# Six of 24 adaLN parts moved from TensorE beside the mixers to ScalarE, GpSimd and VectorE in three FFNs

## The chip, the core and the metric

The kernel runs on one core of one Trainium2 chip. The metric is device time in microseconds of one execution; the kernel before took 2847.01 us (median of three runs, 2842.42 to 2851.52). In the profile PE is TensorE (PEld its weight loads), DVE VectorE, ACT ScalarE, POOL GpSimd, SP SyncE, whose queue issues the DMAs.

## The reference, cut to what matters

One inference step of a four-layer trunk over 128 context tokens and 256 latent tokens, width 1024. Layer i has a mixer (0 and 3: gated DeltaNet, GDN; 1: Mamba-2 SSD; 2: RG-LRU), then a ConvFFN with 2816 hidden channels, twice (gate and value), a 3x3 depthwise convolution and a projection back. Each of these eight sub-layers is modulated:

```python
mod = silu(cond) @ ada_w[l] + ada_b[l]                # cond: 2 rows (latents, context); ada_w[l]: 1024 x 6144
sh1, sc1, g1, sh2, sc2, g2 = jnp.split(mod, 6, -1)
x = layer_norm(ALPHA * x + g1 * mixer(x * (1 + sc1) + sh1), ln_g[0], ln_b[0])
x = layer_norm(ALPHA * x + g2 * ffn(x * (1 + sc2) + sh2), ln_g[1], ln_b[1])
```

A "part" below is one of the six 1024-wide slices of one layer's mod: two rows of 1024 inputs times a 1024 x 1024 weight. There are 24 parts, and each reads 4 MB of weights once.

## The kernel before, in words

All data is fp32. Large products run as three fp32r passes on exact high and low halves (mm3, line 157). A weight tile of 128 x 1024 (512 KB) is therefore prepared in wload (line 137): SP's queue loads it into a ring of raw buffers, ScalarE copies it to the high half (wh, or woh for the FFN's second weight), and GpSimd, sometimes VectorE, subtracts to get the low half (wl, wol). A raw buffer is free again when the subtraction is done.

**Modulation.** ada (line 187) computes one part on TensorE: for each of eight steps it loads a raw tile of 128 x 1024 and multiplies it by a 32-column slice of csilu, the SiLU of the two condition rows (the other 30 columns are zero), in plain fp32, as four products of 256 columns, one for each 32-column group of the array. They accumulate in a PSUM tile psa. At the end VectorE adds the bias (adab); a gate part is stored to a DRAM scratch (gate_rows), a shift or scale part is transposed on TensorE into a psc tile and copied out.

The 24 parts form a list, todo, that is consumed in order; HOSTED (line 28) says how many are computed beside each layer's mixer, its first boundary and its second. Two more are computed at the start. parts() (line 288) takes the next n, and more where a later sub-layer needs them. Beside a mixer the steps are spread evenly over its projections: fill (line 176) is called after each projection, at lines 761, 999 and 1319. Before, the mixers host 6 (GDN, layer 0), 3 (SSD), 3 (LRU) and 2 (GDN, layer 3) parts.

**GDN** (line 1180) advances, in turns (interleave, line 1151), 33 projections, the chain of block inversions and the chunk recurrences, so that TensorE has projections to do while a chain waits for other engines. SSD and LRU are built in the same spirit.

**A boundary** (line 297) is the end of a sub-layer: the last products, the residual and norm, and the next sub-layer's input. The norm's gain and bias are applied to x later, by affine (line 415), in half-width multiplications and additions on VectorE with both inputs in SBUF.

**The FFN** (line 547) goes through 22 slices of 128 gate and 128 value channels. In slice j, for each half: 24 products (8 slices of the input, three passes, 384 columns) into one of two psc buffers; then conv9 (line 531), one ScalarE instruction and ten of VectorE, which read the psc buffer and add into acc. In slices 1 to 6 two instructions of affine go in between. Then ScalarE's SiLU of the gate, VectorE's product g, ScalarE's high half gh, VectorE's low half gl; and out(), 18 products with the weights woh and wol of a slice three steps back, into six PSUM banks (four psa, two psb). Input weights are loaded two tiles ahead (FFN_AHEAD), through three raw buffers. The order on ScalarE is pinned to the program's order in this loop; on the other engines the framework's planner lays the order when the kernel is built, and each engine then runs its own list in order.

Of the kernel before, what the change touches and what calls it, by code (L numbers as in the profile page):

```python
# [15 lines left out]
NT = 384                       # 128 context tokens, then 256 latent tokens  # L16
# [3 lines left out]
NFF = 22                       # 128-wide slices of the FFN's hidden channels  # L20
# [3 lines left out]
FFN_AHEAD = 2                  # weight tiles loaded ahead of the one in use  # L24
FFN_LAG = 3                    # steps from a slice's first product to its last
SIDE = 4, 4, 4
FENCE = 4                      # weight tiles after a boundary that are kept behind it
HOSTED = ((6, 2, 1), (3, 2, 1), (3, 0, 1), (2, 1, 0))     # modulation parts beside each layer's mixer and norms
WBUFS = ((4, 2), (3, 4), (4, 3), (2, 6))     # raw and split weight tiles: GDN, SSD, LRU, FFN

# columns of the constant input
# [37 lines left out]
class Slices:  # L69
    """the parts of a tile that isn't in use yet, as scratch"""  # L70
# [14 lines left out]
class Trunk:  # L85
# [43 lines left out]
    def ln_exp(self):  # L129
        """one table set for both functions, so that they don't evict each other"""  # L130
        self.tables("natural_log_exp_and_others")
# [25 lines left out]
    def mm3(self, out, w, x, start, stop):  # L157
        """out += (wh + wl)^T (xh + xl) without the lo*lo pass"""
        (wh, wl), (xh, xl) = w, x
        self.mm(out, wh, xh, start, False)  # L160
        self.mm(out, wh, xl, False, False)
        self.mm(out, wl, xh, False, stop)
# [13 lines left out]
    def fill(self, share=None):  # L176
        """one step of the products hosted beside a mixer, or up to a share of them"""
# [9 lines left out]
    def ada(self, l, u, raws=None, pool=None):  # L187
        """part u of layer l's modulation (shift, scale, gate of the mixer, then of the FFN): a quarter of the
        features in each column group of the array, one row per condition"""
        nc = self.nc  # L190
# [9 lines left out]
        md = self.sb(pool or self.adap, [128, 256], "adab", 2)  # L200
# [6 lines left out]
        else:  # L207
            pc = self.ps("c")
            for s in range(2):
                self.transpose(pc[:, s * 128:(s + 1) * 128], md[:, s * 128:(s + 1) * 128])  # L210
            mc = self.modc[l, u] = self.sb(self.fix, [128, 8, 2], f"mod{u}", 2)
            nc.vector.tensor_copy(mc.rearrange("p (j s) r -> p s j r", s=2),
                                  pc[:, :256].rearrange("p (s j r) -> p s j r", s=2, j=4)[:, :, :, 0:2])
        yield

    def scales(self, l, which, ln):
        """per-feature columns A, B with h = A*n + B for n the normalized (or raw) input"""
# [30 lines left out]
    def make_h(self, t, n, A, B, pool):  # L248
        """transpose one token tile and write its hi/lo parts feature-major"""
# [18 lines left out]
    def open_bnd(self, l, which):  # L268
        """what the end of a sub-layer needs, loaded ahead"""
# [12 lines left out]
    def beside(self, l, which):  # L282
        """parts of the modulation computed at this boundary"""
        raws = (self.fp, "raw", 3) if which else (self.bp, "araw", (6, 6, 2)[l % 3])
        for part in self.parts(HOSTED[l][1 + which], () if which else ((l, 5), (l + 1, 1))):
            yield from self.ada(*part, raws, self.bp)

    def parts(self, n, need=()):
        """the next parts of the modulation to compute, at least up to those needed"""
# [7 lines left out]
    def boundary(self, l, which, pts, late, n):  # L297
        """the last products by token tile, each followed by x <- LN(alpha*x + gate*m) and the next sub-layer's
        input or the result; x stays without LN's gain and bias until affine()"""
# [25 lines left out]
        def stats(t):  # L325
            """r = alpha * x + gate * m, 1/deviation and -mean/deviation"""
# [7 lines left out]
            mv = self.sb(bp, [128, 4], "bmv", 2)      # mean, variance, 1/deviation, -mean/deviation  # L334
# [80 lines left out]
    def affine(self, lg, lb, eng=None):  # L415
        """x <- x * gain + bias of the norm before, a token tile per step"""
# [17 lines left out]
    def first_pair(self, srcs):  # L434
        """the first two products of a sub-layer, with the last token tile behind the others"""
# [17 lines left out]
    def rsqrt(self, pool, out, v, scale=1.0):  # L453
        """(scale * v + eps)^-1/2 from ln and exp, with one Newton step"""
# [9 lines left out]
    def softplus(self, pool, x, shape, tag):  # L464
        """max(x,0) + log1p(exp(-|x|)), the log1p by its atanh series"""
# [17 lines left out]
    def conv4(self, pt, dst, w, bias=None):  # L483
        """depthwise taps at offsets -1, 0, 1, 2 inside each segment"""
# [23 lines left out]
    def outproj(self, l, nk, wsrc, gety, tail=4, ws=(), swap=False):  # L508
        """the mixer's last projection, through to the FFN's input"""
# [37 lines left out]
    def ffn(self, l):  # L547
# [3 lines left out]
        with tc.tile_pool(name=self.nm("ffn"), bufs=1, reuse_waits="tile") as fp:  # L551
            self.rawp = self.fp = fp
            cw = self.sb(fp, [128, 2 * NFF, 9], "cw")
            self.load(cw, I["ffn_conv"][l])
            apool = tc.tile_pool(name=self.nm("aff"), bufs=1, reuse_waits="tile")
# [21 lines left out]
            for j in range(NFF):  # L577
                accs = []
                for half in range(2):
# [9 lines left out]
                    if j:  # L589
                        next(affine, 0)  # L590
                if j == 7:
                    apool.__exit__(None, None, None)
                if j == NFF - 3:
# [21 lines left out]
    def lru(self, l, j):  # L615
# [3 lines left out]
        with ExitStack() as es:  # L619
            op = es.enter_context(tc.tile_pool(name=self.nm("lru"), bufs=1, reuse_waits="tile"))  # L620
            Iv = self.sb(op, [128, NB, 2, NT], "I")      # input gate, then its product, then the states
# [5 lines left out]
            sm = self.sb(op, [128, NB, 8], "sm")     # gate_b x4, lambda x2, state x2  # L627
            sa = self.sb(op, [128, NB, 2], "sa")
            st = self.sb(op, [128, NB, 2], "st")
            R = None                                     # recurrence gate, then the decay  # L630
# [1157 lines left out]
```

## Time and profile before

| what | us |
|---|---|
| median of three runs | 2847.01 |
| span of the profiled execution, first to last instruction | 2845.4 |
| TensorE busy in it | 2635.5 (93%) |
| VectorE busy | 1943.4 (68%) |
| ScalarE busy | 1340.0 (47%) |
| GpSimd busy | 1283.2 (45%) |
| modulation products from raw tiles, busy union of all | 109.5 |
| mean granted TensorE clock | 0.972 |

The execution's own time is this span and the little that lies outside its first and last instruction; the median of the runs is 1.6 us above the span. The layers' FFNs lie at about 547 to 800, 1255 to 1510, 1800 to 2055 and 2558 to 2810 us, the mixers between them. In group lines, "busy" is the union over a group's instructions (matmuls overlap in the pipeline, so it is less than count times mean), then the mean of one, then the idle time of the engine just ahead and what ended it. A product in plain fp32 leaves two records in the trace, so a step of ada (four products) is eight records.

### The profile page before, as it was taken

The page shows a single profiled execution, that of the slowest core. Times are in us where ns is not written, and L with a number is a line of the kernel's source. Part 1 is how long each engine was busy: PE and PEld are TensorE (multiplying, and loading weights), DVE is VectorE, ACT ScalarE, POOL GpSimd, SP SyncE. Part 2 cuts the span into 40 slices and gives each one's busy share as a digit, 9 for nine tenths or more (in the row PEclk, how much of TensorE's full clock was granted, in tenths as well). Part 3 has the DMA queues.
Part 4 walks back from the last instruction along what each step waited for, and adds up shares of the span by engine and source line. Part 5 has one row for each costly group of instructions (what it writes and reads, how often), then busy time and mean ns, then how long its engine had stood idle before and what let it go on. Part 6 is the DMA issues. An engine that isn't in the chain of part 4 may idle for free. (4 is left out here: it accounts for less than half of the span.)

```text
span 2845.4 us, 43556 instructions
## 1 busy us (share of the span) xinstructions
PE 2635.5 (93%) x16424; PEld 2319.9 (82%) x16424; DVE 1943.4 (68%) x4200; ACT 1340.0 (47%) x2334; POOL 1283.2 (45%) x658
## 2 busy tenths in 40 slices
PE   6999998999997999899999787999989999899997
PEld 3698887799977789679997675899968888778996
DVE  3666545787786677368778776787776564578877
ACT  2455545434443566443444664344345555544443
POOL 1443332356533443335654653456545333335663
PEclk9999999999999999999999989999999999999998
DMA  7522323534454342543445443334443112053442
GB/s 260 170 96 78 107 82 103 201 132 136 148 174 143 113 127 83 188 167 127 134 148 171 160 143 114 112 128 141 160 140 91 53 57 64 30 183 119 150 137 84
DMA packets 114641, 366.45 MB, mean 129 GB/s; under 512 B 13760, under 2 KB 25728, under 8 KB 114432
## 3 DMA queue, kind: packets, MB, share of 16 engines
q1 hardware_dynamic: 114432, 363.67, 38.8%
q8 instruction: 130, 2.13, 0.3%
q14 instruction: 79, 0.65, 0.1%
HBM read 357.78 MB, written 5.84 MB: 128 GB/s over the span
## 5 line engine op out<-in xcount | busy, mean ns | idle before, releaser
L120 POOL TENSOR_TENSOR wl<-raw,wh 128x1024 fp32r<-128x1024 f32 x305 | 736.5, 2425 | 1009.7 <-ACT wh L111 974.5
L105 PE MATMUL psc<-hh,wh 128*128 128x384 f32 x2168 | 758.6, 350 | 38.5 <-DVE acc L117 14.0
L117 DVE SCALAR_TENSOR_TENSOR acc<-psc,cw,acc 128x189 f32<-128x189 f32 (+3 forms) x1680 | 646.1, 412 | 164.5 <-ACT acc L111 131.1
L105 PE MATMUL psc<-hh,wl 128*128 128x384 f32 x2168 | 736.7, 340 | 4.6 <-POOL wl L120 4.1
L105 PE MATMUL psc<-hl,wh 128*128 128x384 f32 x2168 | 735.6, 339 | 0.0
L105 PEld LDWEIGHTS psc<-hh,wh 128*128 128x128 f32 x2168 | 413.0, 190 | 83.8 <-issue 64.2
L111 ACT ACTIVATE wh<-raw 128x1024 fp32r<-128x1024 f32 x345 | 362.6, 1053 | 238.8 <-PE psc L105 53.9
L105 PEld LDWEIGHTS psc<-hh,wl 128*128 128x128 f32 x2168 | 412.3, 190 | 9.3 <-POOL wl L120 5.0
L105 PEld LDWEIGHTS psc<-hl,wh 128*128 128x128 f32 x2168 | 413.3, 191 | 8.1 <-issue 4.7
L120 POOL TENSOR_TENSOR wol<-raw,woh 128x1024 fp32r<-128x1024 f32 x88 | 211.8, 2407 | 160.4 <-ACT woh L111 159.5
L111 ACT ACTIVATE gh<-g 128x384 fp32r<-128x384 f32 x88 | 46.2, 526 | 329.2 <-DVE g L120 329.2
L111 ACT ACTIVATE acc<-psc,cw 128x384 f32<-128x384 f32 x168 | 96.6, 575 | 191.4 <-PE psc L105 191.4
L120 POOL TENSOR_TENSOR PB<-M,cst 128x512 fp32r<-128x512 f32 x96 | 128.7, 1354 | 83.3 <-PE psa L105 79.0
L111 ACT ACTIVATE V<-psa 128x512 fp32r<-128x512 f32 x144 | 85.4, 597 | 144.8 <-PE psa L105 144.4
L105 PE MATMUL psa<-woh,gl 128*128 128x512 f32 x352 | 137.1, 391 | 3.6 <-DVE gl L120 3.6
L105 PE MATMUL psa<-raw,csilu 128*32 128x256 f32 x1216 | 109.5, 422 | 32.3 <-DMA raw<-in_ada_w 32.2
L105 PE MATMUL psa<-wol,gh 128*128 128x512 f32 x352 | 137.6, 391 | 0.0
L105 PE MATMUL psa<-woh,gh 128*128 128x512 f32 x352 | 137.5, 391 | 0.1
L120 DVE TENSOR_TENSOR wl<-raw,wh 128x1024 fp32r<-128x1024 f32 x40 | 53.6, 1340 | 62.1 <-ACT wh L111 62.1
L111 ACT ACTIVATE woh<-raw 128x1024 fp32r<-128x1024 f32 x88 | 92.6, 1053 | 0.0
L105 PE MATMUL psa<-U,W 128*128 128x256 f32 x576 | 91.9, 281 | 0.0
L111 ACT ACT_TABLE_LOAD x60 | 77.0, 1283 | 28.9 <-DVE zT L117 8.1
(336 smaller groups left out, 5155.1 us busy)
## 6 DMA issues: line engine op xcount, KB each, us to landing
raw<-in_ffn_in SPq DMA_DIRECT2D x176, 512.0 KB
raw<-in_ada_w SPq DMA_DIRECT2D x152, 512.0 KB
raw<-in_ffn_out SPq DMA_DIRECT2D x88, 512.0 KB
raw<-in_gdn_in SPq DMA_DIRECT2D x66, 512.0 KB
araw<-in_ada_w SPq DMA_DIRECT2D x40, 512.0 KB
raw<-in_ssd_in SPq DMA_DIRECT2D x25, 512.0 KB
raw<-in_lru_in SPq DMA_DIRECT2D x20, 512.0 KB
raw<-in_gdn_out SPq DMA_DIRECT2D x16, 512.0 KB
```

Source lines behind the costliest of these rows:

```text
L105: return self.nc.tensor.matmul(out, l, r, start=start, stop=stop, skip_group_check=True)
L111: x = self.nc.scalar.activation(out, in_, f, scale=scale, bias=bias, **kw)
L117: return self.nc.vector.scalar_tensor_tensor(out=out, in0=a, scalar=s, in1=b, op0=op0, op1=op1)
L120: return (eng or self.nc.vector).tensor_tensor(out=out, in0=a, in1=b, op=op)
```

## The change

Six parts are taken from the mixers and computed in the FFNs of layers 0, 1 and 2, two in each, by ada_vec. An FFN does one step per slice: the whole 128 x 1024 weight tile is scaled by one condition value per partition, for each of the two conditions, and summed over the eight steps in two SBUF accumulators of 128 x 1024. The scaling is a ScalarE Copy with a scale; the sum is a GpSimd addition, or, for the second condition on odd steps, one VectorE multiply-add with both inputs in SBUF. After eight steps TensorE sums each accumulator over its 128 partitions by eight products with rowsel, a constant matrix that has ones in one column; the rest (ada_finish) is as before. The tile for the next step is loaded as soon as the current one, in a single buffer vraw, has been read. The accumulators and the scaled copy vtmp have one buffer each.

The mixers now host 3, 1, 4 and 0 parts; the boundaries host as many as before.

```diff
-HOSTED = ((6, 2, 1), (3, 2, 1), (3, 0, 1), (2, 1, 0))
+HOSTED = ((3, 2, 1), (1, 2, 1), (4, 0, 1), (0, 1, 0))
+HOSTED_FFN = 2, 2, 2, 0
...
+    def ada_vec(self, parts, pool, fp):
+        nc = self.nc
+        seq = [(l, u, k) for l, u in parts for k in range(8)]
+        def fetch(i):
+            l, u, k = seq[i]
+            raw = self.sb(pool, [128, 1024], "vraw")
+            self.load(raw, self.I["ada_w"][l, k * 128:(k + 1) * 128, u * 1024:u * 1024 + 1024])
+            return raw
+        nxt, acc = fetch(0), None
+        yield
+        for i, (l, u, k) in enumerate(seq):
+            raw = nxt
+            if k == 0:
+                acc = [self.sb(pool, [128, 1024], f"vacc{r}") for r in range(2)]
+            for r in range(2):
+                c = self.csilu[:, k, r:r + 1]
+                if k == 0:
+                    self.act(acc[r], raw, AF.Copy, c)
+                elif r == 1 and k % 2:
+                    self.stt(acc[r], raw, c, acc[r])
+                else:
+                    tmp = self.sb(pool, [128, 1024], "vtmp")
+                    self.act(tmp, raw, AF.Copy, c)
+                    self.tt(acc[r], acc[r], tmp, ALU.add, nc.gpsimd)
+            nxt = fetch(i + 1) if i + 1 < len(seq) else None
+            yield
+            if k == 7:
+                pt = self.ps("c")
+                for r in range(2):
+                    for j in range(4):
+                        self.mm(pt[32 * j:32 * j + 32, :256], self.rowsel[:, r, :], acc[r][:, j * 256:(j + 1) * 256],
+                                r == 0, r == 1)
+                self.ada_finish(l, u, pt, fp)
+                yield
...
@@ ffn
+            vparts = self.parts(HOSTED_FFN[l], () if last else ((l, 5), (self.next_layer(l), 1)))
+            vpool = tc.tile_pool(name=self.nm("adv"), bufs=1, reuse_waits="tile")
+            vp = vpool.__enter__()
+            vec = self.ada_vec(vparts, vp, fp) if vparts else iter(())
...
+                next(vec, 0)
                 if j == 7:
                     apool.__exit__(None, None, None)
+                if j == NFF - 4:
+                    for _ in vec:
+                        pass
+                    vpool.__exit__(None, None, None)
```

In slice 0 only the first tile is fetched; slices 1 to 8 do the steps 0 to 7 of the first part, slice 9 sums its partitions, slices 10 to 17 do the second part, slice 18 sums it. next(vec) stands after both halves' convolutions and ahead of the slice's woh copy. ada_finish is the end of ada, cut out unchanged; beside no longer asks for the parts that a later sub-layer needs, since ffn does.

More of the change, by code (lines that the diff above doesn't have):

```diff
@@ L187, in ada @@
     def ada(self, l, u, raws=None, pool=None):
-        nc = self.nc
         rpool, tag, n = raws or (self.wp, "raw", self.wbufs[0])
@@ L199, in ada, with ada_finish @@
                 yield
-        md = self.sb(pool or self.adap, [128, 256], "adab", 2)
+        self.ada_finish(l, u, pt, pool or self.adap)
+        yield
+    def ada_finish(self, l, u, pt, pool):
+        md = self.sb(pool, [128, 256], "adab", 2)
         self.load(md, self.I["ada_b"][l, u])
@@ L211, in ada @@
             mc = self.modc[l, u] = self.sb(self.fix, [128, 8, 2], f"mod{u}", 2)
-            nc.vector.tensor_copy(mc.rearrange("p (j s) r -> p s j r", s=2),
-                                  pc[:, :256].rearrange("p (s j r) -> p s j r", s=2, j=4)[:, :, :, 0:2])
-        yield
+            self.nc.vector.tensor_copy(mc.rearrange("p (j s) r -> p s j r", s=2),
+                                       pc[:, :256].rearrange("p (s j r) -> p s j r", s=2, j=4)[:, :, :, 0:2])
+    def ada_vec(self, parts, pool, fp):
[7 more added lines that the diff above has]
+        nxt, acc = fetch(0), None
+        yield
+        for i, (l, u, k) in enumerate(seq):
[22 more added lines that the diff above has]
+                yield
     def scales(self, l, which, ln):
@@ L284, in beside @@
         raws = (self.fp, "raw", 3) if which else (self.bp, "araw", (6, 6, 2)[l % 3])
-        for part in self.parts(HOSTED[l][1 + which], () if which else ((l, 5), (l + 1, 1))):
+        for part in self.parts(HOSTED[l][1 + which]):
             yield from self.ada(*part, raws, self.bp)
@@ L1662, in build @@
             self.act(self.csilu[:, :, 0:2], cc, AF.Silu)
+            self.rowsel = self.sb(fix, [128, 2, 32], "rowsel")
+            nc.vector.memset(self.rowsel, 0.0)
+            for r in range(2):
+                nc.vector.memset(self.rowsel[:, r, r:r + 1], 1.0)
             self.X = []
```

## The prediction

> **What bounds the kernel now.** I read the page first, then busy times by stretch, then the waits and the timeline of an FFN.
>
> ```profile
> span 2845.4 us, 43556 instructions
> PE 2635.5 (93%) x16424; PEld 2319.9 (82%) x16424; DVE 1943.4 (68%) x4200; ACT 1340.0 (47%) x2334; POOL 1283.2 (45%) x658
> PE   6999998999997999899999787999989999899997
> ```
>
> TensorE is busy for 93% of the span, and the third line shows that in nearly every fortieth. So work taken off it is worth something where nothing else ends last, and work put beside it costs nothing until another engine becomes the one that ends last. The change touches two kinds of stage, and they answer differently.
>
> *The mixers.* The two GDN layers run the same code with different numbers of hosted modulation products: six parts (48 steps of one weight tile) in layer 0, two (16 steps) in layer 3. That is an experiment already made. Below are four stretches, bounded by the third projection's first product, the eleventh projection's, and the first product of the output projection; first all instructions, then those that read the conditioning tile csilu alone. Columns are stretch, length, busy time of each engine (instructions), clock, DMA share, GB/s.
>
> ```profile
> 62.00:130.50 68.50, 62.19 (x375) 47.80 (x371) 44.03 (x101) 32.17 (x50) 25.03 (x14) 0.95 0.54 181
> 130.50:478.90 348.40, 335.15 (x2633) 297.74 (x2631) 196.56 (x457) 188.90 (x390) 123.53 (x80) 0.98 0.26 87
> 2092.70:2160.80 68.10, 56.82 (x305) 45.28 (x302) 46.51 (x92) 32.11 (x50) 41.90 (x24) 0.92 0.39 126
> 2160.80:2495.90 335.10, 319.64 (x2459) 290.93 (x2457) 193.21 (x455) 187.86 (x389) 123.97 (x81) 0.98 0.18 55
> ...
> 62.00:130.50 68.50, 7.91 (x100) 2.22 (x96) 0.00 (x0) 0.00 (x0) 0.95 0.54 181
> 130.50:478.90 348.40, 22.28 (x256) 6.96 (x256) 0.00 (x0) 0.00 (x0) 0.98 0.26 87
> 2092.70:2160.80 68.10, 3.85 (x38) 0.90 (x34) 0.00 (x0) 0.00 (x0) 0.92 0.39 126
> 2160.80:2495.90 335.10, 7.00 (x78) 1.70 (x78) 0.00 (x0) 0.00 (x0) 0.98 0.18 55
> ```
>
> A step is eight records (four fp32 products, two records each). In the long stretch layer 0 has 256 records, 32 steps; layer 3 has 78, 9.75 steps; the other PE records agree (2377 against 2381). Layer 0 takes 348.40 - 335.10 = 13.3 us longer: 13.3 / 22.25 = 0.60 us a step. In the first stretch it has 12.5 steps against 4.75 and takes 0.4 us longer: 0.05 us a step. There the steps fill holes.
>
> *The FFN.* Two stretches of layer 0's FFN: one in which VectorE also applies the last norm's gain and bias to x (affine), and one late. Then who TensorE waited for in the first.
>
> ```profile
> 585.00:636.00 51.00, 49.42 (x261) 46.10 (x260) 43.36 (x96) 19.27 (x27) 27.32 (x13) 1.00 0.35 117
> 716.00:790.00 74.00, 74.00 (x394) 69.77 (x393) 54.94 (x136) 30.21 (x43) 43.55 (x19) 1.00 0.45 146
> ...
> PE psc L105 <- DVE acc L117: 1.6, 2, 1.0
> ```
>
> Late, TensorE has no gap. In the affine stretch VectorE is busy 43.36 of 51 us, and TensorE waits 1.6 us for its convolution. The ScalarE copies gh, one a slice, show the pace:
>
> ```profile
> 589.21 0.53 ACT L111 ACTIVATE gh<-g 128x384 fp32r<-128x384 f32 x1 [4.24 <-DVE g L120]
> 628.83 0.53 ACT L111 ACTIVATE gh<-g 128x384 fp32r<-128x384 f32 x1 [6.13 <-DVE g L120]
> ...
> 743.99 0.53 ACT L111 ACTIVATE gh<-g 128x384 fp32r<-128x384 f32 x1 [3.91 <-DVE g L120]
> 756.45 0.53 ACT L111 ACTIVATE gh<-g 128x384 fp32r<-128x384 f32 x1 [3.91 <-DVE g L120]
> ```
>
> Late, a slice takes 12.46 us, set by TensorE. In the affine stretch three slices take 39.62, 13.2 each: there VectorE, with ScalarE's answers to it, already sets the pace. I expect the change to be decided in that stretch.
>
> **The change part by part.** *Taken from the mixers.* With the new counts layer 0 hosts three parts, SSD one (before: three), LRU four (three), layer 3 none (two). Layer 0: of its steps, 32 lie in the long stretch; half go, 16 x 0.60 = 9.6, and 8 early ones at 0.05, 0.4: 10.0 us. Layer 3: 9.75 x 0.60 = 5.9, and 6 early ones 0.3: 6.2 us. For SSD and LRU:
>
> ```profile
> 867.00:1100.00 233.00, 13.80 (x160) 3.49 (x160) 0.00 (x0) 0.00 (x0) 0.98 0.43 133
> 1545.00:1700.00 155.00, 15.35 (x192) 4.44 (x192) 0.00 (x0) 0.00 (x0) 0.90 0.49 158
> ...
> PE psb L108 <- DVE ys L797: 14.0, 1, 14.0
> PE psc L105 <- DVE xr L117: 13.5, 4, 5.1
> PE psa L105 <- DMA raw<-in_ada_w: 5.7, 4, 3.0
> ```
>
> SSD: 20 of its 24 steps lie after its one long wait (14.0 us, which ends at 867 and is VectorE's); two thirds go, 13.3 x 0.60 = 8.0 us; the four before the wait are worth nothing. LRU gains 8 steps. It is full of waits for VectorE (13.5 us), which hide a step, and for these very weight tiles (5.7 us), which a step lengthens; between 0.05 and 0.60 I take the middle, 8 x 0.33 = 2.6 us. Mixers together: 10.0 + 6.2 + 8.0 - 2.6 = 21.6 us less. Ends: 12, if the inversions' chain cannot use the time, and 26, if LRU's steps are free and SSD's early ones count.
>
> *TensorE's work in the FFNs.* A part ends in eight products with rowsel, the shape of two steps, back to back:
>
> ```profile
> 288.63 1.07 PE L105 MATMUL psa<-raw,csilu 128*32 128x256 f32 x16
> 289.64 0.44 PE L105 MATMUL psc<-hh,wh 128*128 128x384 f32 x1
> ```
>
> 1.0 us to the next product, six times: 6 us. The two transposes of a part move along and cancel. But the sum now takes one of the two psc buffers, and for three parts the transposes another, from the ring that feeds the convolution, and the transposes wait for VectorE's add, which is queued behind a convolution of ten instructions (nine of them here; the tenth had its own group):
>
> ```profile
> 747.05 3.90 DVE L117 SCALAR_TENSOR_TENSOR acc<-psc,cw,acc 128x127 f32<-128x127 f32 x9 [1.95 <-ACT acc L111]
> ```
>
> The output products can lie over most of that. I take 1 us a part, 6 us; ends 0 and 3.9 each.
>
> *The sixteen steps of an FFN on the other engines.* One step a slice: slices 1 to 8 and 10 to 17. The first of a part is two ScalarE products. An odd one is one ScalarE product, one GpSimd add and one VectorE multiply-add; an even one two ScalarE products and two GpSimd adds. Prices, and what happens when VectorE meets GpSimd:
>
> ```profile
> L120 POOL TENSOR_TENSOR wl<-raw,wh 128x1024 fp32r<-128x1024 f32 x305 | 736.5, 2425 | 1009.7 <-ACT wh L111 974.5
> L111 ACT ACTIVATE wh<-raw 128x1024 fp32r<-128x1024 f32 x345 | 362.6, 1053 | 238.8 <-PE psc L105 53.9
> L120 DVE TENSOR_TENSOR wl<-raw,wh x40: 1208/1225/2747, 468.2 to 2507.3; 128x1024 fp32r<-128x1024 f32 x40
> ...
> 595.49 2.40 POOL L120 TENSOR_TENSOR wol<-raw,woh 128x1024 fp32r<-128x1024 f32 x1
> 604.25 2.41 POOL L120 TENSOR_TENSOR wl<-raw,wh 128x1024 fp32r<-128x1024 f32 x1 [6.37 <-ACT wh L111]
> 745.54 4.91 POOL L120 TENSOR_TENSOR wl<-raw,wh 128x1024 fp32r<-128x1024 f32 x2 [3.39 <-ACT wh L111]
> ...
> 596.21 2.23 DVE L120 TENSOR_TENSOR x<-x,lng 128x512 f32<-128x512 f32 x1
> 601.52 0.68 DVE L120 TENSOR_TENSOR x<-x,lnb 128x512 f32<-128x512 f32 x1
> ```
>
> GpSimd's op runs from 595.49 to 597.89. VectorE's x op, both inputs in SBUF, starts inside it and takes 2.23 us; the like op at 601.52, in GpSimd's idle 6.37 us, takes 0.68. A meeting costs 1.55 us. Convolutions, which read PSUM, don't show it (the nine above took 0.43 each, mostly beside GpSimd's pair at 745.54). The Trainium skill, SBUF — State Buffer, section "SBUF: two separate sides", has the rule: the two engines share a port pair as an exclusive lock, and a VectorE op with two SBUF inputs waits out a whole GpSimd op. The trace agrees. By that rule without the slack below, every new add could be met; that is rival C.
>
> Affine slices (1 to 6) have steps 0 to 5: three odd, two even. VectorE sets the pace, so its additions count in full. Odd: 1.23 for the multiply-add and half a meeting, 2.0 us. Even: two adds fill the 6.37 us in which GpSimd stood idle and g was made unhindered: one meeting, 1.55. 3 x 2.0 + 2 x 1.55 = 9.1 us an FFN, 27 for three; ends 0 and 52 (rivals A and C).
>
> Other slices: late VectorE is busy 54.94 of 74, 3.2 us idle in a slice, over the 2.0 of an odd step. On an even step ScalarE's second product waits for the first add, since vtmp has one buffer: 2 x 1.05 + 2.4 = 4.5 us, and queued behind it stand woh, Silu, gh and the next slice's wh and acc, and TensorE behind these. Its idle 3.91 before gh nearly covers that. GpSimd then has five ops a slice and ScalarE's 1.05 between the adds, 5 x 2.4 + 1.05 = 13.1 against 12.46: 0.6 late, caught up in the odd slice after it (four, 9.6). I take 1 us an FFN, 3 in all; ends 0 and 13.
>
> The 48 weight loads go to SP's queue in the FFNs, each waiting there for its single buffer with three-buffer raw loads behind it. 66 big loads an FFN become 82: a DMA share of 0.45 becomes 0.56, about the 0.54 seen at 62 to 130 us. I cost them at nothing; if a fetch stands ahead of a needed load, up to a few us an FFN, inside C's end. The bias and gate rows move too, small and early.
>
> Sum: -21.6 + 6 + 6 + 27 + 3 = +20.4 us. On this execution's 2845.4 that is 2865.8. The median of the runs, 2847.0, is 1.6 above the span: 2867 us.
>
> **The rivals.** *A, VectorE's holes take it up, faster.* In the affine stretch VectorE idles 7.6 of 51 us, 1.9 a slice, almost what an odd step needs (2.0). If the multiply-add lies in the holes ahead of a convolution and the adds end before g, the affine term is gone, and with half the part ends: -21.6 + 6 + 3 = -12.6, 2834 us. It decides where VectorE's additions stay under 1.9 us a slice. Against it: those holes are mostly waits for ScalarE's gh and acc, in which the next op is not ready.
>
> *B, half of it.* 12 instead of 27 in the affine stretch: -21.6 + 12 + 12 = +2.4, 2849 us, not to be told from no change. For it: the order on each engine is laid anew and can part the two.
>
> *C, every two-input VectorE op meets GpSimd.* GpSimd's share in the affine stretch, 27.32 / 51 = 0.54, grows by seven adds of 2.4 in some 66 us to 0.79. Four such ops a slice and the three multiply-adds, 23, each wait 0.79 x 1.2 = 0.95: 22, less the some 8 they wait now, plus 3.7 of multiply-adds: 17.5 an FFN, 52. With late slices at 13: -21.6 + 12 + 52 + 13 = +55, 2902 us. Against it: GpSimd is idle when ScalarE waits for g, just when g runs.
>
> *D, the mixers gain half.* If the inversions become bound by their chain, 10 instead of 21.6: +32, 2879 us. Against it: 22 steps paid in full between layers 0 and 3; for it: layer 3 is then below anything seen.
>
> **How the numbers follow.** Forecast 0.40 (2867), A 0.18, B 0.25, C 0.10, D 0.07. 0.3%, 8.5 us, is about what a measurement of this kernel can tell from no change: A is faster, B the same, the others slower: 0.18, 0.25, 0.57. The range reaches from A's sum to between D and C: 2834 to 2892; outside lie most of C and A's better half.
>
> **What would show it.** Right: the GDN stretches shorter by some 10 and 6 us and SSD by 8; the three hosting FFNs each longer by 10 to 15 us, layer 3's FFN unchanged; TensorE's wait for acc in 585 to 636 up from 1.6 to about 10; g and x ops of 1.5 to 2.5 us where they took 0.6. Wrong: hosting FFNs that keep their length (A), late slices over 13 us (C), GDN stretches that don't shrink while U and W are waited for (D).

## The result and the profile after

The changed kernel takes 2935.26 us (median of four runs, 2933.72 to 2937.82); beside it, on the same chip, the kernel before took 2848.78. The ratio is 1.031, 95% interval 1.0294 to 1.0326. The direction was forecast (slower, 0.57), the size was not: 2935 lies far outside 2834 to 2892.

The head of the page and TensorE's row of the 40 slices, as shown of before:

```profile
span 2932.4 us, 43102 instructions
PE 2651.7 (90%) x16136; PEld 2342.6 (80%) x16136; DVE 2033.6 (69%) x4227; ACT 1416.3 (48%) x2406; POOL 1443.7 (49%) x718
PE   6999998989897998989989887899889999989997
```

TensorE has 288 records fewer, yet is busy 16 us longer, and its share falls from 93% to 90%. The other three engines took the work without being full: VectorE is at 69%. Where the 87 us of the span went shows when each sub-layer is measured, in the trace, from the last weights product of the one before to its own:

| us | before | after | difference | forecast |
|---|---|---|---|---|
| GDN, layer 0 | 518.7 | 514.7 | -4.0 | -10.0 |
| FFN, layer 0 | 300.0 | 335.1 | +35.1 | +14 |
| SSD | 409.0 | 392.9 | -16.1 | -8.0 |
| FFN, layer 1 | 300.0 | 335.8 | +35.8 | +14 |
| LRU | 243.3 | 250.1 | +6.8 | +2.6 |
| FFN, layer 2 | 298.9 | 329.5 | +30.6 | +14 |
| GDN, layer 3 | 467.7 | 464.9 | -2.8 | -6.2 |
| FFN, layer 3, to the end | 307.8 | 309.3 | +1.5 | 0 |

The mixers gave 16.1 us, of 21.6 forecast. The three hosting FFNs grew by 101.5, of 42 forecast: 59.5 of the 66.6 us by which the forecast missed the span's growth (87.0 against 20.4). Below are the stretches whose like was shown of before (columns as there): the affine one, the late one, and inside the late one a few us around one gap.

```profile
585.00:636.00 51.00, 45.55 (x231) 41.84 (x230) 42.05 (x82) 21.39 (x28) 38.28 (x16) 0.97 0.44 145
716.00:790.00 74.00, 61.90 (x295) 58.05 (x294) 56.90 (x115) 30.67 (x40) 55.47 (x23) 0.88 0.43 139
...
716.00:722.50 6.50, 2.00 (x9) 1.34 (x8) 6.36 (x16) 1.11 (x2) 6.50 (x4) 0.88 0.63 206
722.50:728.00 5.50, 5.50 (x18) 5.50 (x19) 3.50 (x8) 1.94 (x3) 2.51 (x2) 0.52 0.56 184
728.00:734.00 6.00, 6.00 (x35) 5.91 (x34) 3.23 (x8) 1.97 (x3) 4.11 (x2) 1.00 0.26 87
```

The late stretch, where TensorE had no gap at all, is the surprise: it is busy 61.90 of 74 us there, at a granted clock of 0.88. The last three rows show both losses. TensorE is idle for 4.5 of 6.5 us; then it is busy, but does 18 products in 5.5 us where the next 6 us hold 35: the clock is at 0.52 after the gap.

What lies ahead of that gap, engine by engine (start, us, and in brackets the idle time before and what ended it). VectorE:

```profile
709.93 1.49 DVE L121 TENSOR_TENSOR g<-acc,acc 128x384 f32<-128x384 f32 x1 [1.16 <-ACT acc L112]
712.30 2.47 DVE L118 SCALAR_TENSOR_TENSOR vacc<-vraw,csilu,vacc 128x1024 f32<-128x1024 f32 x1 [0.88 <-DMA vraw<-in_ada_w]
714.69 2.77 DVE L121 TENSOR_TENSOR gl<-g,gh 128x384 fp32r<-128x384 f32 x1
717.38 6.78 DVE L118 SCALAR_TENSOR_TENSOR acc<-psc,cw,acc 128x127 f32<-128x127 f32 x18
```

GpSimd, ScalarE's second scaled product, SP's fetch of the tile, and TensorE:

```profile
708.62 2.39 POOL L121 TENSOR_TENSOR vacc<-vacc,vtmp 128x1024 f32<-128x1024 f32 x1 [1.27 <-ACT vtmp L112]
710.97 2.71 POOL L121 TENSOR_TENSOR wol<-raw,woh 128x1024 fp32r<-128x1024 f32 x1
713.64 6.04 POOL L121 TENSOR_TENSOR wl<-raw,wh 128x1024 fp32r<-128x1024 f32 x2
...
707.38 1.16 ACT L112 ACTIVATE vtmp<-vraw,csilu 128x1024 f32<-128x1024 f32 x1 [2.52 <-POOL vacc L121]
...
708.57 0.33 SPq L135 DMA_DIRECT2D vraw<-in_ada_w  x1
...
722.50 0.66 PE L106 MATMUL psc<-hh,wh 128*128 128x384 f32 x1 [4.50 <-DVE acc L118]
```

Read it in this order. ScalarE's product waits 2.52 us for vtmp, so the next tile is only asked for at 708.57. The planner had placed the next step's multiply-add on VectorE right behind g, ahead of gl and of the next convolution; VectorE, which takes its list in order, waits there 0.88 us for the tile. Then it meets GpSimd's wol (2.47 us instead of 1.28), and gl meets wl (2.77 instead of 0.56; the kernel before has g and gl like this):

```profile
602.12 0.55 DVE L120 TENSOR_TENSOR g<-acc,acc 128x384 f32<-128x384 f32 x1
603.26 0.56 DVE L120 TENSOR_TENSOR gl<-g,gh 128x384 fp32r<-128x384 f32 x1 [0.59 <-ACT gh L111]
```

The convolution begins at 717.38, though both of ScalarE's starting values stood ready by 714.82 (the second was begun at 714.25 and took 0.57). TensorE has used up its 18 output products and waits 4.5 us for a psc buffer. None of the three delays is long. Together they are longer than what TensorE has in stock. This is one gap read closely; what the chain is worth over the whole kernel is for the experiments to say.

The same waits over this whole FFN, 520 to 850 us (total, times, longest). The first was 3.1 us, three times, in the kernel before:

```profile
PE psc L106 <- DVE acc L118: 24.7, 13, 4.6
ACT vtmp L112 <- POOL vacc L121: 17.3, 6, 3.6
DVE vacc L118 <- DMA vraw<-in_ada_w: 8.1, 5, 3.1
```

### The profile page after: what moved, and what is told of

Its sections match the earlier page's. It is cut to its first block, busy times and chain, and to the rows that moved or that the text cites. A ratio compares the mean times of both kernels' runs of the same rounds, so it can differ in the third digit from the quotient of the medians.

```text
span 2932.4 us, 43102 instructions
## 1 busy us (share of the span) xinstructions
PE 2651.7 (90%) x16136; PEld 2342.6 (80%) x16136; DVE 2033.6 (69%) x4227; ACT 1416.3 (48%) x2406; POOL 1443.7 (49%) x718
## 5 line engine op out<-in xcount | busy, mean ns | idle before, releaser
L121 POOL TENSOR_TENSOR wl<-raw,wh 128x1024 fp32r<-128x1024 f32 x305 | 747.9, 2463 | 907.4 <-ACT wh L112 873.5
L106 PE MATMUL psc<-hh,wh 128*128 128x384 f32 x2168 | 770.9, 356 | 109.1 <-DVE acc L118 76.3
L106 PE MATMUL psc<-hh,wl 128*128 128x384 f32 x2168 | 745.4, 344 | 4.8 <-POOL wl L121 4.8
L106 PE MATMUL psc<-hl,wh 128*128 128x384 f32 x2168 | 745.5, 344 | 0.0
L106 PEld LDWEIGHTS psc<-hh,wh 128*128 128x128 f32 x2168 | 421.6, 194 | 155.4 <-issue 138.9
L106 PEld LDWEIGHTS psc<-hl,wh 128*128 128x128 f32 x2168 | 421.9, 195 | 6.4 <-issue 4.4
L121 POOL TENSOR_TENSOR vacc<-vacc,vtmp 128x1024 f32<-128x1024 f32 x60 | 143.3, 2389 | 35.4 <-ACT vtmp L112 35.2
L106 PE MATMUL psa<-raw,csilu 128*32 128x256 f32 x832 | 77.6, 432 | 34.0 <-DMA raw<-in_ada_w 33.9
L121 DVE TENSOR_TENSOR gl<-g,gh 128x384 fp32r<-128x384 f32 x88 | 73.4, 834 | 41.5 <-ACT gh L112 41.5
L112 ACT ACTIVATE woh<-raw 128x1024 fp32r<-128x1024 f32 x88 | 92.5, 1051 | 13.3 <-DMA raw<-in_ffn_out 13.2
L121 DVE TENSOR_TENSOR g<-acc,acc 128x384 f32<-128x384 f32 x88 | 82.4, 936 | 16.7 <-ACT acc L112 10.6
```

What stands on the lines that cost most here:

```text
L106: return self.nc.tensor.matmul(out, l, r, start=start, stop=stop, skip_group_check=True)
L112: x = self.nc.scalar.activation(out, in_, f, scale=scale, bias=bias, **kw)
L121: return (eng or self.nc.vector).tensor_tensor(out=out, in0=a, in1=b, op=op)
```

## The experiments

Two theories stood at the start: the additions of VectorE and GpSimd meet in SBUF (L), or the single buffers vtmp and vraw make a chain of waits (B). The texts on record name further ones (T, O, S, G, H) as they came up. For all kernels below, one table of the profiled executions. It has the growth of one hosting FFN against before (mean of three), of its parts as paced by the copies gh (slice 0 to 7 "early", 7 to 18 "late"), and, per FFN, the time TensorE waited for a convolution, ran at half its clock, and VectorE stood still ahead of multiply-adds; then the change of all mixers and the last FFN together. The half clock is counted from the clock's changes in the trace, whether TensorE is busy in it or not.

| kernel | FFN | early | late | TensorE waits | half clock | VectorE waits | rest |
|---|---|---|---|---|---|---|---|
| before | 0 | 0 | 0 | 3.4 | 6.8 | 0 | 0 |
| after | +33.8 | +13.7 | +19.0 | 24.6 | 26.2 | 8.1 | -14.6 |
| a_no_sums | +2.3 | 0.0 | +1.6 | 3.3 | 5.7 | 0 | -10.0 |
| b_no_multiply_add | +15.0 | +6.7 | +8.1 | 14.2 | 6.8 | 0 | -14.0 |
| c_no_gpsimd_adds | +8.4 | +8.1 | +1.7 | 8.6 | 3.4 | 9.2 | -15.5 |
| d_two_vtmp | +28.9 | +16.7 | +13.7 | 21.8 | 19.3 | 8.0 | -15.0 |
| j_two_vraw | +44.5 | +20.3 | +28.4 | 31.8 | 42.1 | 16.7 | -9.1 |
| e_half_adds | +37.6 | +15.1 | +22.0 | 22.1 | 30.7 | 10.4 | -11.5 |
| f_all_vector | +42.8 | +23.6 | +24.6 | 32.8 | 35.3 | 9.3 | -9.7 |
| k_all_gpsimd | +35.5 | +14.4 | +19.4 | 28.7 | 15.9 | 0 | -14.9 |
| i_step_last | +33.6 | +12.4 | +29.1 | 23.0 | 23.9 | 0 | +12.3 |
| l_every_second | +25.4 | +10.4 | +13.8 | 19.0 | 20.5 | 7.8 | -8.5 |
| m_half_step | +9.0 | +4.6 | +5.2 | 8.0 | 9.1 | 5.1 | -14.8 |
| m_pinned | +16.0 | +10.4 | +13.2 | 6.2 | 10.2 | 0 | +7.7 |
| n_half_pinned | -0.4 | -0.8 | +7.3 | 1.3 | 5.7 | 0 | -0.9 |
| o_half_gpsimd | +3.2 | +1.0 | +1.4 | 4.1 | 9.1 | 0 | -2.8 |
| p_before_pinned | -5.4 | -3.1 | +2.9 | 1.0 | 3.4 | 0 | +18.8 |

A row is one execution. Those of m_half_step and n_half_pinned are the shortest of their kernels, 6 and 9 us under the median; those of o_half_gpsimd and m_pinned are the longest, 9 and 10 us above it.

**Parts of the work alone.** Without any sum beyond the first products:

```diff
-            for r in range(2):
+            for r in range(2 if k == 0 else 0):
```

> Steps 1 to 7 of the moved parts are left out (their weight tiles are still loaded, nothing reads them); step 0's two ScalarE products, the row sums on TensorE and the part ends stay. Theory L (VectorE's two-input SBUF instructions wait out GpSimd's new adds) and theory B (single buffers: ScalarE waits for vtmp, VectorE for vraw) both say that the loss goes: mixers -16, row sums +6, part ends 0 to +6, so 2837 to 2845 us. If the loads on SP's queue or the taken psc buffers were the cost, it stays above 2870.

It took 2844.51 us, a single execution as for all kernels here without an interval (before on that chip: 2852.51); its span is 2842.4, 3 below before's. What is left, loads and part ends, costs 2.3 us an FFN. So even with the sums free the change could bring no more than some 3 to 8 us.

Without the multiply-adds (their line becomes a pass), and without GpSimd's additions (their line goes):

```diff
-                    self.stt(acc[r], raw, c, acc[r])
+                    pass
...
-                    self.tt(acc[r], acc[r], tmp, ALU.add, nc.gpsimd)
```

> VectorE's multiply-add on odd steps is left out; ScalarE's products and GpSimd's adds stay. Theory L: half of the 101 us that the three FFNs grew by, since the multiply-add waits in front of gl, but g and gl still meet GpSimd: 2875 to 2895 us. Theory B: only VectorE's 8 us an FFN of waiting for vraw and the 1.2 us each go, ScalarE's wait for vtmp stays: 2900 to 2915.

> GpSimd's adds are left out; ScalarE still writes its products (nothing reads them) and VectorE keeps its multiply-adds. Theory L and B both: no new meetings and no wait for vtmp; what stays is the multiply-adds in the affine slices (3 x 2 us an FFN) and vraw: 2855 to 2875 us. If the multiply-add alone were the cost, it stays above 2900.

They took 2878.16 and 2856.89 us (2852.51). Over the floor of 2.3 the one half costs 12.7 us an FFN and the other 6.1; both together cost 31.5. Both times lie in the ranges that L gave (B gave the second's too). But the work is no sum of its parts, and neither theory said so: each half finds room that it doesn't find when the other stands there.

**The buffers.** A second vtmp, and a second vraw; in both, g has one buffer instead of two to make room, which is a change too:

```diff
-                    tmp = self.sb(pool, [128, 1024], "vtmp")
+                    tmp = self.sb(pool, [128, 1024], "vtmp", 2)
...
-            raw = self.sb(pool, [128, 1024], "vraw")
+            raw = self.sb(pool, [128, 1024], "vraw", 2)
```

> The whole computation, with two buffers for vtmp (and one for g, whose readers are done in time, to make room). Theory B: ScalarE's wait for GpSimd's add (17.3 us in one FFN) goes and with it 10 us or more an FFN: 2890 to 2905 us. Theory L: GpSimd does the same adds and VectorE meets them as before: 2920 to 2940.

> The whole computation, with two buffers for vraw (one for g), so that the next tile is loaded before ScalarE is done with the one in use. The multiply-add's waits for vraw (24 us in three FFNs) go. If that wait is what makes gl late, 2900 to 2915; if the meetings with GpSimd are, 2925 to 2940.

2918.99 (2852.51) and 2971.53 (2853.47). ScalarE's wait for vtmp is gone in the first, and the FFN is 4.9 us shorter, no more. The second is worse than the change, and above every range expected. VectorE's g starts without a wait in both, so its single buffer is not seen to cost anything. With the tile there early, VectorE waits for GpSimd's addition into the same accumulator instead; this is j's row of VectorE's waits, 550 to 860 us, and its group of multiply-adds (shortest, median, longest, ns):

```profile
DVE vacc L118 <- POOL vacc L121: 17.0, 6, 3.7
```

```profile
L118 DVE SCALAR_TENSOR_TENSOR vacc<-vraw,csilu,vacc x24: 1285/3343/3361, 556.5 to 2121.4; 128x1024 f32<-128x1024 f32 x24
```

When it may go at last, GpSimd has begun its next operation, and most multiply-adds take 3.34 us instead of 1.28. B falls as the main cause.

**The additions' shape and engine.** GpSimd's additions in two halves of 512 columns; all additions as VectorE multiply-adds; all of them on GpSimd:

```diff
-                    self.tt(acc[r], acc[r], tmp, ALU.add, nc.gpsimd)
+                    for h in (slice(0, 512), slice(512, 1024)):
+                        self.tt(acc[r][:, h], acc[r][:, h], tmp[:, h], ALU.add, nc.gpsimd)
...
-                elif r == 1 and k % 2:
+                elif True:      # f_all_vector; False: k_all_gpsimd
```

> The whole computation; each GpSimd add is cut into two of 512 columns, so GpSimd does the same work in instructions of half the length. Theory L (an instruction of VectorE with two SBUF inputs waits for the end of the GpSimd instruction it meets): the waits on g, gl and the multiply-add get shorter, the FFNs grow by 22 to 27 us each instead of 34, 2900 to 2915 us. Theory T (GpSimd's sheer load makes weights or adds late): nothing gained, 2930 to 2945.

> The whole computation; all fourteen sums of a part after step 0 are multiply-adds on VectorE, no GpSimd add and no vtmp. Theory L: the new GpSimd instructions that were met are gone, but VectorE gets 17 us a part: in the affine slices, where it sets the pace, all of it counts (10 to 15 us an FFN), in the late ones 2.5 us a slice fit into its 3.2 of idle time: 2875 to 2900 us. If VectorE's own load is what counts (four multiply-adds alone cost 8.4 us an FFN, fourteen then some 29): 2910 to 2935.

> The whole computation; all fourteen sums of a part after step 0 are GpSimd adds, no multiply-add on VectorE. Without the multiply-adds ten adds a part cost 13 us an FFN over the floor; fourteen make every slice an even one (five GpSimd instructions, 13.1 us against TensorE's 12.46): 18 to 25 us an FFN, 2895 to 2920, below the changed kernel, if the pair of multiply-add and adds is what costs. If GpSimd's load is what costs, above it: 2940 or more.

2948.61 (2849.08), 2966.10 (2849.08) and 2938.64 (2853.47): all as bad as the change or worse, the first two above every range expected. Shorter operations to wait behind don't help, nor does it to take the sums from GpSimd altogether, or from VectorE. In k ScalarE waits for vtmp instead, because GpSimd has five operations of 2.4 us in a slice that takes TensorE 12.5 (its waits, 520 to 870 us):

```profile
ACT vtmp L112 <- POOL vacc L121: 63.1, 14, 5.3
```

L alone falls too; meetings are one of several ways to be late.

**The step's place in the slice.** The step behind gl instead of ahead of woh, so that ScalarE's woh, SiLU and gh go first:

```diff
-                next(vec, 0)
...
                 self.split(gh, gl, g)
...
+                next(vec, 0)
```

> The whole computation; the step of a slice is called behind gl instead of ahead of the woh copy, so that on ScalarE its products stand behind gh, and in the program its multiply-add behind gl. Theory O (what makes the two halves cost more together than apart is the order: the multiply-add stands ahead of gl, waits for vraw and for GpSimd, and gl then meets wl): the three late TensorE waits of 3 to 4.6 us an FFN go and with them the halved clock: FFNs grow by 15 to 22 us instead of 34, 2880 to 2900. Theory L by the number of meetings alone: as many instructions meet, 2920 to 2940.

2960.20 (2853.47). This is above every range expected. Meetings of g and gl are gone but for those that before has too: the time that the 132 of them take beyond 0.56 us each is 9.7 us over the three FFNs, 57.4 in the change and 7.9 before. No multiply-add waits, and the FFN is as long as in the change: 12 early, 29 late. The multiply-adds, now in the middle of convolutions, take a median of 3.18 us, beside GpSimd nearly all the time.

**The mixers alone**, in the kernel before: two of SSD's parts, then also one of LRU's, to layer 0's GDN.

```diff
-HOSTED = ((6, 2, 1), (3, 2, 1), (3, 0, 1), (2, 1, 0))
+HOSTED = ((8, 2, 1), (1, 2, 1), (3, 0, 1), (2, 1, 0))     # g
+HOSTED = ((9, 2, 1), (1, 2, 1), (2, 0, 1), (2, 1, 0))     # h
```

> The kernel before with another distribution and nothing else: two parts that SSD hosted go to layer 0's GDN mixer (8, 1, 3, 2 beside the mixers). From the mixers of the changed kernel: SSD 14 to 16 us shorter; GDN longer by 16 steps, at 0.17 us as 24 fewer steps there showed (3 us) or at 0.60 as layers 0 and 3 showed (10 us). 4 to 13 us below the kernel before, ratio 0.995 to 0.999.

> As the other distribution, and one more part from LRU to layer 0's GDN mixer (9, 1, 2, 2). LRU grew by 6 to 13 us with 8 steps more, so with 8 fewer it may give 5 to 8; GDN takes 1.4 to 5 more. 7 to 17 us below the kernel before if LRU's price holds downwards; no better than the other one if LRU's steps only cost when they are added.

Ratios 0.9994 (0.9984 to 1.0005) and 1.0023 (1.0009 to 1.0036). The gain expected is not there: SSD is 12.6 us shorter, and GDN 11.5 longer for 16 steps more (0.72 a step). LRU is 5.1 us longer in g though it hosts what it did.

**How much in a slice.** One part in each FFN (mixers 5, 1, 3, 2): a whole step in every second slice, or half a step, one condition, in every slice.

```diff
-HOSTED_FFN = 2, 2, 2, 0
+HOSTED_FFN = 1, 1, 1, 0
...
-                next(vec, 0)
+                if j == 0 or j % 2:          # l_every_second
+                    next(vec, 0)
...
+                if r == 0:                   # m_half_step, at the end of the loop over r
+                    yield
```

> One part in each of three FFNs instead of two, a whole step in every second slice (slices 1, 3, ... 15); the mixers host 5, 1, 3 and 2 parts. Slack theory (S): a slice has some 2 to 3.5 us that nothing needs, a step costs by how far it overruns the slice it stands in, and what is overrun is lost, so a step costs what it does in the changed kernel: 31.5 us over the floor for 16 steps, 2.0 a step, 16 for 8 and 1 for the part's end: 17 us an FFN, in all 51 less 14 to 16 in SSD and 1 to 4 in layer 0: 2881 to 2889 on the time before of this chip. Lag theory (G): an overrun is made up in the next slice when that has no step: under 8 us an FFN, 2845 to 2862.

> The same parts in the same places, but half a step in a slice (one condition's product and sum, the other condition's in the next slice; 16 slices, one part). S: each half fits into the slack of its slice, as the halves alone did (6 us without GpSimd's additions, 13 without the multiply-adds, for two parts): half of these or less, 3 to 6 us an FFN with the part's end: 2838 to 2855. G: the same load in twelve of every sixteenth slices over the same time as in every second slice, so the same cost, to 2 us an FFN. If both kernels cost 15 us or more an FFN, neither theory holds, and a cost per addition that does not depend on what stands beside it remains.

Ratios 1.0229 (1.0214 to 1.0245) and 1.0071 (1.0053 to 1.009). The same 8 steps cost 25.4 us an FFN whole and 9.0 in halves. Half the steps, whole, cost three quarters of what 16 cost, and the empty slice in between gives little back. It is what a single slice must hold that counts (S), more so than expected (17 and 3 to 6; both times lie above the ranges of S). In m what is left comes in every fourth slice, and VectorE's timeline shows why:

```profile
1379.85 1.50 DVE L118 SCALAR_TENSOR_TENSOR vacc<-vraw,csilu,vacc 128x1024 f32<-128x1024 f32 x1 [1.46 <-DMA vraw<-in_ada_w]
1381.27 0.85 DVE L118 SCALAR_TENSOR_TENSOR acc<-psc,cw,acc 128x192 f32<-128x192 f32 x2
```

By the program this multiply-add belongs two slices later. The planner put it ahead of the last two instructions of a convolution, where its tile had not come: 3 us in which the convolution stands.

**The order on VectorE.** In the FFNs convolutions and multiply-adds keep the program's order among themselves: on the changed kernel (m_pinned), on m_half_step (n), on before as the control (p). And m_half_step without any multiply-add, all sums by ScalarE and GpSimd (o).

```diff
 def stt(...):
-        return self.nc.vector.scalar_tensor_tensor(out=out, in0=a, scalar=s, in1=b, op0=op0, op1=op1)
+        x = self.nc.vector.scalar_tensor_tensor(out=out, in0=a, scalar=s, in1=b, op0=op0, op1=op1)
+        if self.pinned:
+            self.tc.keep_in_program_order(x)
+        return x
...
-                elif r == 1 and k % 2:
+                elif False:                  # o_half_gpsimd
```

> The changed kernel; in the FFNs VectorE's convolutions and multiply-adds (the scalar_tensor_tensor instructions) keep the program's order among themselves, so that no multiply-add stands inside a convolution ahead of its weight tile. Early-placement theory (H): the idle time ahead of the multiply-adds (24 us over the three FFNs in the changed kernel) and the waits of TensorE that follow it go, with their halved clock: 8 to 20 us an FFN less, 2875 to 2915. Load theory (S): a whole step overruns its slice wherever it stands: within 4 us an FFN of the changed kernel, 2920 to 2950.

> m_half_step with the same pinned order. H: of its 9 us an FFN, 1.2 are the part's end and most of the rest follows a multiply-add that waits 1.5 us for its tile inside a convolution (2.5 us in every fourth slice, slices 2, 6, 10, 14); these go: 3 to 5 an FFN, 2838 to 2855. S: as m_half_step, 2858 to 2872.

> m_half_step without multiply-adds: the second condition's odd steps are a ScalarE product and a GpSimd addition too, so VectorE has none of the added work and GpSimd one addition in each of 14 slices (four operations of 2.4 us, 9.6 of the slice's 12.5). H: 3 to 5 us an FFN, 2838 to 2855. If meetings of g, gl and the norm's operations with GpSimd's additions are what costs: 6 to 12 an FFN, 2855 to 2875.

> The kernel before with the pinned order alone, the control for the two pinned kernels: within 3 us of before. If it is slower or faster by more, the pinned kernels are read against this one.

| kernel | median us | before on that chip | ratio, 95% interval |
|---|---|---|---|
| m_pinned | 2892.80 | 2847.04 | 1.0150 (1.0127 to 1.0172) |
| n_half_pinned | 2854.08 | 2847.04 | 1.0021 (1.0010 to 1.0031) |
| o_half_gpsimd | 2845.05 | 2847.04 | 0.9991 (0.9979 to 1.0003) |
| p_before_pinned | 2848.11 | 2847.04 | 0.9999 (0.9989 to 1.0010) |

(m_pinned's profiled execution took 2902.92 us, the longest of its four.) The control is no different in time from before, so the pin by itself explains nothing (it shortens the FFNs, by 5.4 us each, and lengthens the rest by 18.8). On the changed kernel it takes away half of the loss: 3.1% becomes 1.5%, 41 of 86 us. The meetings are not what went: beyond 0.56 us each for g and gl and 1.27 for a multiply-add, these instructions take 71.4 us more over the three FFNs in the change and still 63.0 in m_pinned (7.9 before). What makes up the other half was not taken apart by a run. Here are slices 0 to 7 and 7 to 18 of layer 1's FFN: before, after, m_pinned and o_half_gpsimd.

```profile
1262.48:1350.02 87.54, 84.42 (x445) 78.41 (x444) 73.31 (x166) 34.53 (x50) 50.16 (x21) 1.00 0.40 130
1350.02:1477.92 127.90, 127.90 (x685) 120.93 (x684) 97.48 (x242) 54.52 (x78) 78.84 (x33) 1.00 0.43 140
```

```profile
1277.39:1379.29 101.90, 90.44 (x461) 82.30 (x460) 82.80 (x170) 45.85 (x61) 73.14 (x30) 0.98 0.44 144
1379.29:1527.70 148.41, 134.89 (x697) 124.48 (x696) 119.01 (x253) 68.15 (x91) 109.18 (x44) 0.93 0.46 147
```

```profile
1267.67:1366.15 98.48, 90.61 (x458) 81.77 (x457) 83.78 (x169) 45.70 (x61) 73.18 (x30) 0.98 0.46 149
1366.15:1507.52 141.37, 137.32 (x740) 125.66 (x739) 119.64 (x253) 68.03 (x90) 108.75 (x45) 1.00 0.49 157
```

```profile
1253.24:1342.31 89.07, 85.07 (x440) 79.08 (x439) 73.27 (x166) 41.77 (x56) 64.05 (x26) 0.98 0.42 137
1342.31:1471.45 129.14, 129.14 (x700) 121.30 (x699) 104.60 (x243) 63.33 (x86) 99.84 (x42) 1.00 0.49 160
```

In the late slices of the changed kernel TensorE idles 13.5 of 148.41 us and runs at 0.93 of its clock; with the order kept it idles 4.1, at 1.00. (Its stretch is still 13.5 us longer than before's, and some 6 of these are output products, 27 more of 0.23 us, that before do not come until after slice 18.) And with half a step in a slice and none of it on VectorE, GpSimd works 99.84 of 129.14 us there, a larger share than in the change, and TensorE has no gap. (It does 14 additions an FFN there, 20 in the change.) GpSimd's busy share alone does not tell the loss; what stands in another's way within a slice does not show in it.

No kernel beats before by more than the interval: o's median is 2.0 us below, inside its interval. In its profiled execution, the longest of twelve, the half of the parts costs 3.2 us an FFN, and the mixers and the last FFN give only 2.8 in all, because LRU is 8.8 us longer.

## Why the prediction was wrong

**The step that failed: "Other slices ... I take 1 us an FFN".** Slices 8 to 18 grew by 19.0 us an FFN, 1.6 of which are part ends (a_no_sums). The working was one of busy time: VectorE "3.2 us idle in a slice, over the 2.0 of an odd step", ScalarE's chain hidden by its "idle 3.91 before gh", GpSimd's 0.6 of lateness "caught up in the odd slice after it". Each sum holds on its engine. But each slack was spent as if the others were still there: ScalarE late for vtmp makes the fetch late, the fetch VectorE, VectorE's convolution TensorE, all within one slice. The runs show that it is the combination that costs: over the floor 6.1 and 12.7 us for the halves, 31.5 for both. The chain itself is read off one gap; d_two_vtmp, which takes its first link away, gains only 4.9 us. And a late slice did not catch up in the next: l_every_second.

**The multiply-add was never given a place.** It was priced at 1.23 us and half a meeting, as if it ran when ready. The prediction notes that "the order on each engine is laid anew" only as a hope, for B. In the trace VectorE waits 8.1 us an FFN ahead of multiply-adds and stands in a convolution's way; m_pinned, which changes that order alone, is 17.8 us an FFN shorter than the change, 12.4 more than the pin makes the FFN of before shorter. "I cost them at nothing", said of the weight loads, failed with it: the DMA share is as low as forecast or lower (0.43 late), but the one fetch that VectorE stands behind is issued late.

**The clock was not in the sum at all.** It forecast waits of 10 us in a stretch and charged them once. TensorE's waits of 3.0 us and more for a convolution, eleven in the three FFNs (3.0 to 4.6 us), each go with 3.4 or 6.8 us at half clock that begin within the wait or up to 1.1 us behind it. Per FFN that is 19.4 us more than before. TensorE is busy in 21.2 us of half clock, 5.6 before: 15.5 us more, 7.8 us of lost time. With 21.2 of waits and the 2.3 of the floor this makes 31.3 of 33.8; the rest is not placed. Over the FFNs of layers 0 to 2 in all kernels here, 67 of 67 such waits of 3.5 us and more went with a stretch at half clock that began within them or up to 1.5 us behind, 14 of 22 from 3.0 to 3.5, 28 of 54 from 2 to 3, and 3 of 145 from 1 to 2.

**Right, or right in kind.** *The affine slices:* 9.1 us an FFN forecast; slices 0 to 7 grew by 13.7. Of that 4.2 lie in the first slice alone (10.3 to 14.5 us between copies gh), which had been costed at nothing: there the first multiply-add waits for its tile (below). The rest is 9.5. The wait for acc in 585 to 636 was to go from 1.6 to about 10; it is 5.4, the clock 0.97. The x and g operations of 1.5 to 2.5 us are there (timeline of VectorE after):

```profile
560.72 1.28 DVE L118 SCALAR_TENSOR_TENSOR vacc<-vraw,csilu,vacc 128x1024 f32<-128x1024 f32 x1 [3.06 <-DMA vraw<-in_ada_w]
...
614.84 2.21 DVE L121 TENSOR_TENSOR x<-x,lnb 128x512 f32<-128x512 f32 x1
620.73 2.75 DVE L121 TENSOR_TENSOR g<-acc,acc 128x384 f32<-128x384 f32 x1
```

*The meeting price* of 1.55 us was too low for a full wait: 2.75 against 0.56 is 2.2. *Part ends:* 4 us an FFN forecast with the transposes' wait, at most 2.3 measured. *Layer 3's FFN:* 1.5 us.

*The mixers* gave 5.5 us less than forecast in sum, by errors that partly cancel. In layer 0 the first 16 steps of the long stretch, priced at 0.60, were worth nothing (after: the two long stretches, then TensorE's waits in the first):

```profile
125.80:474.60 348.80, 330.09 (x2506) 297.99 (x2506) 197.51 (x454) 188.70 (x389) 124.71 (x82) 0.96 0.20 62
2255.40:2584.90 329.50, 313.70 (x2350) 291.36 (x2349) 189.12 (x441) 187.78 (x387) 122.08 (x80) 0.96 0.14 41
```

```profile
PE psa L106 <- DVE U L121: 5.2, 3, 2.8
PE psa L106 <- DVE W L121: 4.0, 2, 2.7
```

The stretch is as long as before (348.40) with 128 records less, and the waits for U and W, 2.5 and 2.7 us before, have grown: rival D, true in layer 0. The clock is lower too: half for 27.3 us of it, 17.1 before. In layer 3 the long stretch lost 5.6 us for 9.75 steps, 0.57 each, as forecast, though the half clock there grew from 13.7 to 27.3 us, and the early stretch gave 2.5 back. Net, a step taken out gave 0.17 us in layer 0 and 0.18 in layer 3, and one added to the 48 (g) cost 0.72: the difference of two layers gave the price at the top, and it was carried down to where a step costs little. SSD gave 1.0 a step instead of 0.60; it was 6 to 16 us shorter, mostly 12 to 16, in the kernels that host one part there. LRU's +6.8 can't be put down to its eight steps: it was 5 to 9 us longer in g, l, m_half_step, n, o and p, which host three parts there as before. What makes it so was not settled.

*The rivals.* A and B, the faster and the even one, needed VectorE's work to lie in holes; with the planner's order it made holes. C was right that the late slices cost ("late slices at 13", in all; they took 57), but its reason does not carry it: with the adds halved or the pairing gone (e, f, k) the time stayed, and in i_step_last it stayed without the meetings of g and gl.

The Trainium skill, TensorE: Matmul & The Clock Gate, section "HAM oscillation — how this bites in real kernels", warns of TensorE idle gaps over about 3.4 us. The trace agrees in kind, and here gaps from 3.0 us on did it: 3.0 to 4.6 us, each with 3.41 or 6.83 us at half clock. The forecast asked how much the gaps add up to and not how long each is; 7.8 us in each of three FFNs, 23 of the 87, hang on that.

## What to carry to other kernels

Idle time on four engines adds up to room only if no engine hands its lateness to the next within the same turn of the loop: give an added step less than the smallest slack of one turn (here half a step cost 9.0 us an FFN or less and the same work in whole steps 25.4), and don't expect the next turn to repair it. Ask of every instruction added to an engine that works in order where it will stand in the list and whether its data is there by then; one that waits inside a chain costs the chain, whatever the engine's busy share. Price gaps of a TensorE loop by their length: in these runs waits of 1 to 2 us almost always cost their sum alone, and every one of 3.5 us and more a stretch at half clock as well.

## What the runs showed of the hardware

- A meeting in SBUF costs both sides. When the multiply-add waits for GpSimd's operation (712.30, 2.47 us), GpSimd's next one starts late as well: of the pair at 713.64, which takes 4.8 us alone, 6.04. The Trainium skill, SBUF — State Buffer, section "SBUF: two separate sides", has the exclusive lock; the trace shows it handed to and fro, and GpSimd's wl and wol take 22.5 us beyond 2.40 us each over the three FFNs, 3.2 before.
- ScalarE's product with a scale per partition took 1.14 us where its plain copy of the same tile takes 1.05; the prediction used the latter for both.
- A shorter operation on GpSimd didn't shorten the others' waits: in e_half_adds the multiply-adds took a median of 2.60 us, 1.64 in the change (1.27 at best in both).
